# Four buffers instead of two for the stored expert activations that a transformer block reads back

## The chip, the cores and the metric

The kernel runs on one core of one Trainium2 chip. The metric is the device time of one execution in microseconds (us), as a median over runs; the span of a profile is the time from the first to the last instruction on the core. The core has five engines that run at the same time and meet only through semaphores: TensorE (PE: matmuls, with its weight loads shown as PEld), VectorE (DVE), ScalarE (ACT), GpSimd (POOL) and SyncE (SP, which here only issues transfers). Each engine, and each queue on which an engine issues transfers (SPq, POOLq), works strictly in its own order: an instruction that waits holds up everything behind it.

## The reference, cut to what matters

One layer of a hybrid encoder on 512 tokens of width 1024: two kinds of attention, then a feed-forward part made of 16384 single-neuron experts of which each token picks 8 x 16, then a gated embedding. The change touches the expert part alone:

```python
def peer_ffn(h, w_query, sub_keys, expert_u, expert_v):   # h: 512 x 1024
    ...                                                   # scores, top 16 per head -> eidx, g
        u = jnp.take(expert_u, eidx, axis=0)
        a = jnp.einsum('thkd,td->thk', u, hc).astype(jnp.float32)
        act = (jax.nn.gelu(a, approximate=False) * g).astype(hc.dtype)
        vv = jnp.take(expert_v, eidx, axis=0)
        return jnp.einsum('thk,thkd->td', act, vv)
```

## The kernel before

The first 128 tokens are done as the reference writes it: GpSimd gathers rows of `peer_expert_u` and `peer_expert_v` (`experts0`, L920 to L951; tile `gath`, three buffers), and VectorE does one fused multiply per gathered tile. This work runs beside everything else.

The other 384 tokens are done densely, over 128 blocks of 128 experts. For one block b:

- *up* (`up`, L1010 to L1021): 24 matmuls give the pre-activations `aT` (128 experts x 384 tokens), from the block of `uT` (512 KB, load L130, split into a rounded high part by ScalarE L141 and a low part `wl` by VectorE L143). ScalarE applies Gelu into a tile `ge`.
- *act* (`act`, L1130 to L1144): VectorE multiplies the activations by the block's gate matrix `G` (L1139), ScalarE rounds the product (`ahi`, L1141), VectorE takes the rest (`alo`, L1143). `ahi` and `alo` have three buffers each. `G` comes from DRAM for four blocks at a time (768 KB, L1133, two buffers).
- *down* (`down`, L1146 to L1154): 18 matmuls (L1153) of `ahi` and `alo` with the block of `peer_expert_v` (512 KB, load L130, split in the same way into `vh` by ScalarE and `vl` by VectorE; two raw and three split buffers), summed up over all 128 blocks in six PSUM banks `out`.

The gate matrices are not ready until late. So the ups of blocks 0 to 75 (`NSP` = 76) are done early, beside the selection work, and their activations are stored to DRAM (`ahead`, L1037; `ge_d`, 192 KB a block). After that a last stage, called the **fused stage** here, goes through all 128 blocks in the order of the list `order` (L1023): groups of four *fresh* blocks (up, act, down) alternate with one or two groups of four *stored* blocks, for which the activation is read back from `ge_d` into a tile `gr` (L1136, L1137) and only act and down remain. There are 52 fresh and 76 stored blocks. The act of a block is written one block ahead of its down (list `pend`, L1162).

A tile's tag with `bufs=2` has two places. A load into a place may go out only when the last reader of what lay there is done: for `gr` that is the subtraction L1143 two stored blocks earlier. The program text is not the final order. A planner simulates the kernel, gives each engine and queue a fixed order from its own costs, and sets the semaphores; a load gets its place on SP's queue about where the simulation sees its buffer come free. The loads of the last stage (`gple`, `x3` from `x2_d`, `pl` from `ple_d`; L1184 to L1214) are tied behind the load of `G` that is current twelve blocks before the end (`late`, L1170), so that they come onto SP's queue while the last stored blocks still run.

Of the kernel before, what the change touches and what calls it, by code (L numbers as in the profile page):

```python
# [10 lines left out]
F32 = mybir.dt.float32  # L11
# [53 lines left out]
def block_kernel(ctx: ExitStack, tc: tile.TileContext, a: dict):  # L65
# [26 lines left out]
    def mark(i):  # L92
        latest[:] = [i.ins]
        return i
# [1029 lines left out]
    dn = dns.enter_context(tc.tile_pool(name="dn", bufs=1))  # L1124
# [5 lines left out]
    def act(b, ge):  # L1130
        if b % GB == 0:
            Gs[:] = [dn.tile([128, 384 // TH, GB, TH], F32, tag="G", name="G", bufs=2)]
            loads[:] = [nc.sync.dma_start(Gs[0], g_d[:, :, b:b + GB].rearrange("s p b t -> p s b t")).ins]  # L1133
        G = Gs[0][:, :, b % GB]
        if ge is None:
            ge = dn.tile([128, 384], F32, tag="gr", name="gr", bufs=2)  # L1136
            nc.sync.dma_start(ge, ge_d[b])  # L1137
        gv = ge.rearrange("p (s t) -> p s t", t=TH)
        mark(nc.vector.tensor_mul(gv, gv, G))  # L1139
        ahi = dn.tile([128, 384], F32R, tag="ahi", name="ahi", bufs=3)  # L1140
        nc.scalar.copy(ahi, ge)  # L1141
        alo = dn.tile([128, 384], F32R, tag="alo", name="alo", bufs=3)
        nc.vector.tensor_sub(alo, ge, ahi.bitcast(F32))  # L1143
        return ahi, alo  # L1144
# [11 lines left out]
    def whole(b):  # L1156
        for v in up(b):
            if isinstance(v, float):
                tick(v)
        return v  # L1160

    pend = []  # L1162
    for i, (b, fresh) in enumerate(order):
        if i == GB * HEAD:

            exp_side.rate = left[0] / (sum(3.88 * f + 3.84 for _, f in order[i:]) - EARLY)
        ge = whole(b) if fresh else None
        pend.append(act(b, ge))
        if i == NB - 12:
            late = loads[0]  # L1170
        if len(pend) > 1 and i <= NB - 3:
            run(down(*pend.pop(0), i - 1, V.take(1)))
            V.free()
# [115 lines left out]
```

## Time and profile before

| what | value |
|---|---|
| median of three runs | 1824.28 us (1823.26 to 1829.8) |
| the profiled execution's own time | 1824.99 us |
| span in its profile | 1823.2 us |
| TensorE busy over the span | 1781.7 us (98%) |
| VectorE, ScalarE, GpSimd busy | 1311.8 us (72%), 727.6 us (40%), 537.1 us (29%) |
| fused stage | about 1012 to 1756 us of the span, then the last projection to the end |

Busy time is the time in which an engine executes something. Idle time is listed in front of the instruction that follows it, with what ended it. Matmuls overlap in TensorE's pipeline, so that the duration of one (0.39 us in the fused stage) is longer than the distance between two.

### The profile page before, as it was taken

To read this page: it belongs to the slowest core of one execution; us is meant where nothing else is said; L and a number is where in the kernel's file an instruction comes from. 1 tells how busy PE (TensorE), PEld (TensorE's weight loads), DVE (VectorE), ACT (ScalarE), POOL (GpSimd) and SP (SyncE) were. 2 spreads that over 40 slices of the span, in tenths; PEclk is the share of its full clock that TensorE was granted. 3 is DMA by queue.
4 is the path that set the end of the run, shared out by engine and by line. 5 is a ranking of instruction groups with operands and counts; after the bars stand their busy time and mean duration, and the time that the engine had idled before them with its cause. 6 is when DMAs were issued, how large, how long until landed. Compare 5 with 4: busy or idle time off the path is not lost.

```text
span 1823.2 us, 26237 instructions
## 1 busy us (share of the span) xinstructions
PE 1781.7 (98%) x9613; PEld 1562.5 (86%) x9613; DVE 1311.8 (72%) x2638; ACT 727.6 (40%) x1202; POOL 537.1 (29%) x428
## 2 busy tenths in 40 slices
PE   8999999999899899999999999999999999999998
PEld 6997777788788799999999988888787888888787
DVE  6634644436568899998998678777786887778664
ACT  4434553443333545444444433333333333333342
POOL 4201111112434121132452134333343433344200
PEclk9999999999899999999999999999999999999999
DMA  5231124334312576788888989898898999899922
GB/s 183 81 92 35 47 54 127 93 108 135 127 47 93 187 265 196 258 276 324 307 323 329 363 317 342 320 334 325 299 338 309 329 349 331 318 329 327 354 98 81
DMA packets 159537, 417.12 MB, mean 229 GB/s; under 512 B 14128, under 2 KB 61488, under 8 KB 156336
## 3 DMA queue, kind: packets, MB, share of 16 engines
q1 hardware_dynamic: 122112, 279.64, 44.3%
q0 software_dynamic: 36864, 134.23, 20.3%
q8 instruction: 75, 1.23, 0.3%
q10 hardware_dynamic: 432, 1.57, 0.2%
q14 instruction: 54, 0.44, 0.1%
HBM read 368.73 MB, written 45.88 MB: 227 GB/s over the span
## 4 chain that ended last, share of the span: by engine, by line
PE 75%; DMA 11%; issue 6%; DVE 4%; POOL 2%; ACT 1%; SPq 0%; POOLq 0%; DVEq 0%; ACTq 0%
PE out L1153 14%; PE aT L171 8%; PE aT L172 8%; PE aT L173 8%; DMA gath<-peer_expert_v,eidx 4%; PE gp L1103 4%; PE proj L171 3%; DMA gr<-ge_d 3%; PE proj L172 3%; PE proj L173 3%; POOL gath L932 2%; PE gt L173 2%; PE gt L171 2%; PE gt L172 2%; PE qp L171 2%
## 5 line engine op out<-in xcount | busy, mean ns | idle before, releaser
L171 PE MATMUL aT<-hhi,wh 128*128 128x384 f32 x1024 | 345.7, 338 | 4.8 <-ACT ge L1020 4.8
L173 PE MATMUL aT<-hhi,wl 128*128 128x384 f32 x1024 | 345.0, 337 | 0.0
L172 PE MATMUL aT<-hlo,wh 128*128 128x384 f32 x1024 | 344.7, 337 | 0.0
L141 ACT CAST wh<-wr 128x1024 fp32r<-128x1024 f32 x216 | 226.8, 1052 | 238.2 <-PE aT L172 160.8
L932 POOL DMA_INDIRECT gath<-peer_expert_u,eidx x128 | 185.9, 1453 | 434.0 <-DVE gath L943 292.5
L143 DVE TENSOR_TENSOR wl<-wr,wh 128x1024 fp32r<-128x1024 f32 x184 | 228.2, 1241 | 107.0 <-ACT wh L141 104.5
L932 POOL DMA_INDIRECT gath<-peer_expert_v,eidx x128 | 197.2, 1541 | 306.8 <-DVE acc L951 224.3
L1153 PE MATMUL out<-vh,ahi 128*128 128x512 f32 x768 | 233.1, 392 | 9.2 <-ACT ahi L1141 9.2
L1153 PE MATMUL out<-vl,ahi 128*128 128x512 f32 x768 | 238.4, 392 | 3.4 <-DVE vl L143 3.3
L1153 PE MATMUL out<-vh,alo 128*128 128x512 f32 x768 | 233.4, 391 | 2.1 <-DVE alo L1143 2.1
L141 ACT CAST vh<-vr 128x1024 fp32r<-128x1024 f32 x128 | 134.4, 1051 | 224.6 <-DMA vr<-peer_expert_v 174.3
L171 PEld LDWEIGHTS aT<-hhi,wh 128*128 128x128 f32 x1024 | 193.0, 189 | 8.1 <-ACT ge L1020 5.2
L951 DVE SCALAR_TENSOR_TENSOR acc<-gath,act,acc 128x1024 f32<-128x1024 f32 x128 | 163.9, 1280 | 44.1 <-DMA gath<-peer_expert_v,eidx 43.8
L172 PEld LDWEIGHTS aT<-hlo,wh 128*128 128x128 f32 x1024 | 192.9, 188 | 3.0
L173 PEld LDWEIGHTS aT<-hhi,wl 128*128 128x128 f32 x1024 | 192.9, 188 | 1.6
L943 DVE SCALAR_TENSOR_TENSOR gath<-gath,h2n 128x1024 f32<-128x1024 f32 x128 | 155.1, 1219 | 32.0 <-DMA gath<-peer_expert_u,eidx 31.7
L1153 PEld LDWEIGHTS out<-vh,ahi 128*128 128x128 f32 x768 | 143.1, 188 | 37.5 <-ACT ahi L1141 11.3
L1153 PEld LDWEIGHTS out<-vl,ahi 128*128 128x128 f32 x768 | 143.8, 188 | 35.8 <-DVE vl L143 6.0
L149 POOL TENSOR_TENSOR wl<-wr,wh 128x256 fp32r<-128x256 f32 x128 | 99.6, 815 | 250.6 <-ACT wh L141 220.8
L1153 PEld LDWEIGHTS out<-vh,alo 128*128 128x128 f32 x768 | 143.6, 188 | 34.7 <-DVE alo L1143 4.6
L143 DVE TENSOR_TENSOR vl<-vr,vh 128x1024 fp32r<-128x1024 f32 x128 | 156.1, 1220 | 11.8 <-ACT vh L141 11.7
L171 PE MATMUL proj<-wh,hhi 128*128 128x512 f32 (+1 forms) x256 | 108.6, 427 | 6.8 <-ACT wh L141 6.8
(259 smaller groups left out, 2847.0 us busy)
## 6 DMA issues: line engine op xcount, KB each, us to landing
vr<-peer_expert_v SPq DMA_DIRECT2D x128, 512.0 KB
wr<-uT SPq DMA_DIRECT2D x128, 512.0 KB
g_d<-stage SPq DMA_DIRECT2D x24, 1024.0 KB
G<-g_d SPq DMA_DIRECT2D x32, 768.0 KB
wr<-w_in SPq DMA_DIRECT2D x46, 512.0 KB
ge_d<-ge SPq DMA_DIRECT2D x76, 192.0 KB
gr<-ge_d SPq DMA_DIRECT2D x76, 192.0 KB
wr<-peer_w_query SPq DMA_DIRECT2D x16, 512.0 KB
```

What stands on the lines that cost most here:

```text
L141: nc.scalar.copy(hi, self.raw[i])
L143: nc.vector.tensor_sub(lo, self.raw[i], hi.bitcast(F32))
L149: nc.gpsimd.tensor_sub(l[:, cs], r[:, cs], h[:, cs].bitcast(F32))
L171: nc.tensor.matmul(ps, st[0], mv[0], start=start, stop=False)
L172: nc.tensor.matmul(ps, st[0], mv[1], start=False, stop=False)
L173: nc.tensor.matmul(ps, st[1], mv[0], start=False, stop=stop)
L932: nc.gpsimd.indirect_dma_start(out=t, out_offset=None, in_=a["peer_expert_" + kind], in_offset=bass.IndirectOffsetOnAxis(ap=eidx[:, c:c + ...
L943: nc.vector.scalar_tensor_tensor(t, t, 1.0, h2n, op0=ALU.mult, op1=ALU.mult, accum_out=a0[:, c:c + 1])
L951: nc.vector.scalar_tensor_tensor(acc0, t, act0[:, c:c + 1], acc0, op0=ALU.mult, op1=ALU.add)
L1103: nc.tensor.matmul(gpb[:, 128 * x:128 * x + 128], o[:, 1, cs], m[:, s, cs], start=(s == 0), stop=(s == 2))
L1153: nc.tensor.matmul(outs[t][h], w[:, cs], x[:, h], start=first and p == 0, stop=last and p == 2)
```

## The change

The tag of the tile `gr` gets four places instead of two. Nothing else in the program text differs; the planner runs again over the whole kernel. A place takes 1.5 KB of each partition, so the pool `dn` grows by 3 KB a partition.

```diff
         if ge is None:
-            ge = dn.tile([128, 384], F32, tag="gr", name="gr", bufs=2)
+            ge = dn.tile([128, 384], F32, tag="gr", name="gr", bufs=4)
             nc.sync.dma_start(ge, ge_d[b])
```

## Rows read from the trace of the kernel before

**Rows 1.** Windows: busy us (x instructions) per engine, granted clock, DMA share, GB/s
```profile
core 0: us, PE busy (x) PEld busy (x) DVE busy (x) ACT busy (x) POOL busy (x), PEclk, DMA share, GB/s
1012.00:1756.00 744.00, 729.33 (x3453) 631.41 (x3452) 571.76 (x737) 265.72 (x367) 271.02 (x199) 1.00 0.91 325
```
**Rows 2.** Waits of TensorE, fused stage: waiter <- releaser, total us, times, longest
```profile
PE out L1153 <- ACT ahi L1141: 9.2, 6, 3.1
PE out L1153 <- DVE vl L143: 3.3, 4, 1.5
PE out L1153 <- DVE alo L1143: 2.1, 2, 1.6
```
**Rows 3.** Waits of VectorE in the fused stage
```profile
DVE gr L1139 <- DMA gr<-ge_d: 63.8, 29, 9.8
DVE acc L951 <- DMA gath<-peer_expert_v,eidx: 39.8, 24, 3.9
DVE gath L943 <- DMA gath<-peer_expert_u,eidx: 25.6, 17, 3.2
```
**Rows 4.** Timeline of VectorE, 1278 to 1285 us: start, us, what [idle before]
```profile
1277.56 0.55 DVE L1143 TENSOR_TENSOR alo<-gr,ahi 128x384 fp32r<-128x384 f32 x1
...
1284.57 0.56 DVE L1139 TENSOR_TENSOR gr<-gr,G 128x384 f32<-128x384 f32 x1 [4.77 <-DMA gr<-ge_d]
```
**Rows 5.** Timeline of SP's queue, same stretch
```profile
1278.14 0.33 SPq L1137 DMA_DIRECT2D gr<-ge_d  x1
```
**Rows 6.** Waits of SP's queue in the fused stage
```profile
SPq L130 <- DVE vl L143: 296.0, 118, 7.4
...
SPq L1137 <- DVE alo L1143: 68.7, 37, 7.8
```
**Rows 7.** Chain that ended last: start, us, what
```profile
1045.46 4.12 PE out L1153 x18
```
**Rows 8.** Timeline of TensorE: three of its twelve waits in the stage
```profile
1229.10 0.73 PE L1153 MATMUL out<-vh,alo 128*128 128x512 f32 x2 [0.50 <-DVE alo L1143]
...
1465.19 0.73 PE L1153 MATMUL out<-vh,ahi 128*128 128x512 f32 x2 [0.97 <-ACT ahi L1141]
...
1697.35 0.75 PE L1153 MATMUL out<-vh,ahi 128*128 128x512 f32 x2 [3.06 <-ACT ahi L1141]
```
**Rows 9.** Timeline of VectorE: multiplies that waited ahead of those three
```profile
1223.66 1.03 DVE L1139 TENSOR_TENSOR gr<-gr,G 128x384 f32<-128x384 f32 x2 [2.01 <-DMA gr<-ge_d]
...
1464.03 0.56 DVE L1139 TENSOR_TENSOR gr<-gr,G 128x384 f32<-128x384 f32 x1 [3.87 <-issue]
...
1696.14 0.56 DVE L1139 TENSOR_TENSOR gr<-gr,G 128x384 f32<-128x384 f32 x1 [9.77 <-DMA gr<-ge_d]
```
**Rows 10.** Timeline of SP's queue near the end of the stage
```profile
1643.15 1.99 SPq L1137 DMA_DIRECT2D gr<-ge_d  x2
...
1678.41 1.69 SPq L1191 DMA_DIRECT2D x<-x_d  x3
1680.20 1.01 SPq L1137 DMA_DIRECT2D gr<-ge_d  x1
```
**Rows 11.** Timeline of TensorE after the longest wait
```profile
1697.91 1.04 PE L1153 MATMUL out<-vl,ahi 128*128 128x512 f32 x2
...
1701.31 0.63 PE L1153 MATMUL out<-vh,alo 128*128 128x512 f32 x2
```
**Rows 12.** Windows of short stretches, columns as in the first group
```profile
1698.00:1700.00 2.00, 2.00 (x6) 1.55 (x5) 1.29 (x3) 1.00 (x2) 1.01 (x1) 0.50 0.48 150
...
1509.00:1524.00 15.00, 15.00 (x70) 12.74 (x69) 9.75 (x12) 3.44 (x5) 3.42 (x5) 1.00 0.94 335
...
1250.00:1292.00 42.00, 41.29 (x192) 34.81 (x191) 29.55 (x44) 13.55 (x20) 12.53 (x10) 1.00 0.83 296
1479.00:1509.00 30.00, 30.00 (x150) 26.88 (x149) 27.54 (x41) 13.06 (x19) 13.14 (x10) 1.00 1.00 372
```
**Rows 13.** Waits of ScalarE in the fused stage
```profile
ACT vh L141 <- DMA vr<-peer_expert_v: 174.3, 63, 8.8
```

## The prediction

> **What bounds the kernel now.** I read the page first (TensorE busy 98% of the span), then the windows of the fused stage, the only place where a tile `gr` exists. Of its 744 us TensorE is idle for 744 - 729.33 = 14.67 us [rows 1]. The waits say what that idle time is: matmuls of the down projection that wait for `ahi`, `vl` or `alo`, 9.2 + 3.3 + 2.1 = 14.6 us in 6 + 4 + 2 = 12 places [rows 2]. So the stage is bound by TensorE, and what better buffering can give is bounded: 14.67 us, 0.8% of the kernel, plus what a wait costs after it has ended (below). The reader should set against it the third view, VectorE's waits: 63.8 us in 29 places for a load of `gr`, its largest wait, ahead of the gathers' 39.8 and 25.6 us [rows 3]. Most of these 63.8 us cost nothing now, since act runs a block ahead of down; the whole question is which of the twelve places stand behind them.
>
> The fourth view shows why VectorE waits. A subtraction of an older stored block ends at 1277.56 + 0.55 = 1278.11 us [rows 4]; the load goes out at 1278.14 [rows 5]; the multiply that needs it stands ready from 1279.80 and starts at 1284.57, after 4.77 us idle [rows 4]. The load takes about 6.4 us from issue to use and could not go out sooner, because its place was full. It is the rule: SP's queue stood 37 times, 68.7 us in all, at a load of `gr` until a subtraction had freed the place [rows 6]; 76 such loads, taken in pairs, have 38 occasions.
>
> **The change, part by part.**
>
> *Lead of the load.* A down is 18 matmuls in 4.12 us [rows 7]. With two places a load leads its use by two stored blocks, 2 x 4.12 = 8.2 us, less what passes between a block's multiply and the end of its subtraction (0.56 and 0.55 us [rows 4], and ScalarE's cast and other work between them; I estimate 2 us in all): some 6 us, against a load that takes 6.4 us and more. With four places the lead is 4 x 4.12 = 16.5 us, some 14 after the same deduction. In a group of four stored blocks all four loads can go out during the fresh blocks before it; in a pair of groups the first four can. The 29 waits should nearly all go.
>
> *What of that is on TensorE's path.* I followed each of the twelve waits back through VectorE and ScalarE. Behind six of them stands a late `gr`: the multiply came after a wait of its own, and `ahi`, `alo` or `vl` queued behind it came late for TensorE. The six are 0.50, 0.71, 0.97, 0.57, 0.44 and 3.06 us, in order of time (the first, third and sixth are shown [rows 8]), sum **6.25 us**; the waits of 2.01, 3.87 and 9.77 us on VectorE belong to the three shown [rows 9]. The one of 3.87 us is labelled as issue time; I count it, as it stands at a multiply of a `gr` whose load had just been freed. The other six, 14.6 - 6.25 = 8.35 us, stand behind late loads of `vr`, late gathers or late `G`; I count nothing for them and keep 8.35 us as the bound.
>
> *The longest one.* The load that went out at 1680.20 us was queued on SP behind three loads of `x3` [rows 10] and was used only at 1696.14, 15.9 us later [rows 9]. With four places it is freed where the pair at 1643.15 us was [rows 10], well before `x3` is issued. What is late next? The load two blocks on takes its place behind `x3` and lands around 1696 us; TensorE wanted the first at 1697.35 - 3.06 = 1694.29 [rows 8] and will want that one 2 x 4.12 = 8.2 us later, at 1702.5. Its act needs an estimated 2 us, so about 4 us are left over. I take the whole 3.06.
>
> *The clock after it.* The granted clock was 0.50, the 1.2 GHz level, from 1698 to 1700 us [rows 12], right after TensorE had stood for 3.06 us. Eight matmuls took 1701.31 - 1697.91 = 3.40 us [rows 11]; at 4.12 / 18 each they take 1.83. So that wait cost **1.57 us** more. The five other waits of the six are under 1 us; I charge them nothing.
>
> *Sum.* 6.25 + 1.57 = 7.8 us. The profiled execution took 1824.99 us, 1.79 above its span and 0.71 above the median of the runs; a difference carries over, so 1824.28 - 7.8 = **1816.5 us**. At the most 14.67 + 1.57 = 16.2 us, 1808.0; from below nothing, or a loss (rivals).
>
> *What it adds.* No instruction and no byte. At the stage's start four loads go out at once instead of two, 2 x 192 KB = 0.39 MB more ahead of the others, at 325 GB/s [rows 1] 1.2 us. I take nothing, since the same bytes leave the stretches in which stored blocks run; bound 1.2 us if that cover is gone. The pool's 3 KB shift later tiles; their loads would have to move by far more than these 15 us to matter at the end of the stage. Nothing.
>
> *A rule against my bound.* In a stretch without any wait, 1509 to 1524 us, weight loads are busy for 12.74 of 15 us, 85% [rows 12], and in the whole stage for 631.41 of 744, again 85% [rows 1]. The Trainium skill (Perfetto Trace Analysis, Identifying the Most-Contended Engine) says that busy matmul time is a poor measure of the room left, and that the busy share of weight loads is a good one. By that the room would be 744 - 631.41 = 112.6 us, and the time could fall to 1711.7. The trace does not bear that out: 85% is what it shows where TensorE waits for nothing.
>
> **The rivals.**
>
> *More goes than the six.* VectorE, freed of up to 63.8 us, does its part of the gathers and the splits sooner, `vr` is loaded sooner, and the other waits shrink too. For it: SP's loads wait 296 us for VectorE's `vl` [rows 6]. Against: those waits come from transfers in part, and an earlier VectorE then waits for them. With half of the 8.35 us more: 1816.5 - 4.2 = 1812.3; with all of it 1808.
>
> *No change.* The transfers are the limit: the loads of `gr` come earlier, those of `vr`, `G` and the gathers correspondingly later, and TensorE waits as before; or the planner leaves the loads where they are. 1824, give or take 3. For it: the 16 engines are 0.91 busy over the stage [rows 1], 1.00 at 372 GB/s in one stretch [rows 12], and ScalarE already waits 174.3 us for `vr` [rows 13]. Against: from 1250 to 1292 us, where VectorE stood still for 4.77 us at one `gr` alone [rows 4], the engines were only 0.83 busy [rows 12]: there a place was lacking and not bandwidth. The Trainium skill (HBM Reference, Specifications (TRN2)) gives about 358 GB/s as a core's share when both of a pair stream, and 425 alone. By the first the stage would be 91% full, which is the rival; the 372 GB/s of the trace are above it.
>
> *Slower.* The planner puts the loads of `gr` further ahead on SP's queue than VectorE frees their places on the chip, and `vr` and `wr` wait behind them. The price is the time in which SP stands at such a load, now 37 times for 68.7 us [rows 6], of which TensorE's waits for `vl`, 3.3 us [rows 2], are all that can be seen. If the gain stays, the kernel gets slower by over 0.5% once 9.1 + 7.8 = 16.9 us of it reach TensorE, a quarter. With a third, 22.9 us, it takes 1816.5 + 22.9 = 1839. Against: a place four blocks old is freed earlier than one two blocks old, and the five buffers of `v` cover short stops.
>
> **How the numbers follow.** A measurement of this kernel tells about 0.5%, 9.1 us, from no change, so faster is below 1815.2 and slower above 1833.4. The forecast (a gain of 3 to 9.1 us, 1815.2 to 1821) 0.45; more than the six, past 9.1 us, 0.28; no change 0.15; slower 0.10; the 112.6 us 0.02. Faster 0.28 + 0.02 = 0.30, same 0.45 + 0.15 = 0.60, slower 0.10. The range goes from 1808, the bound of the gain, to 1829, the no-change case with its runs' spread; it leaves out the slower case and the 112.6 us, 0.12.
>
> **What the profile after would show.** VectorE's wait for loads of `gr` falls from 63.8 us to under 15. Waits on SP's queue at L1137 remain, but at places four blocks old. TensorE's idle time in the fused stage falls from 14.67 to about 8 us, the wait of 3.06 near 1697 us and the stretch at half clock behind it are gone, and the six others remain. I am wrong if the waits for `gr` go and TensorE's idle time stays (no change), if new waits for `vl` or `wl` appear behind loads that SP held up (slower), or if the order of other instructions comes out so differently that the twelve places cannot be found again.

## The result, and the profile after

The kernel with four places takes **1807.12 us** (median of 4 runs, 1804.0 to 1809.38) against 1826.38 us (4 runs, 1823.26 to 1829.8) for the kernel before on the same chip: ratio **0.988**, 95% interval 0.9858 to 0.9903, a gain of about 19 us. That is below the forecast of 1816.5 us and just below the range (1808 to 1829). The profiled execution took 1807.68 us with a span of 1805.7; the one of before took 1824.99.

The windows of the fused stage, columns as in [rows 1]. The window is 18 us shorter and holds the same 3453 matmuls as the 744 us of before:

```profile
1012.00:1738.00 726.00, 723.57 (x3453) 631.50 (x3452) 573.52 (x737) 265.85 (x366) 254.85 (x199) 1.00 0.93 333
1690.00:1700.00 10.00, 10.00 (x46) 8.34 (x45) 7.69 (x9) 2.84 (x5) 3.24 (x4) 1.00 1.00 375
```

TensorE's idle time in it is 726.00 - 723.57 = 2.43 us, against 14.67. The second line covers the time at which before had its longest wait and the clock of 0.50 [rows 12]. The same work comes up to 18 us earlier now, but neither is found anywhere in the stage: its longest wait is 1.1 us, and the trace has no stretch at 0.50 in it. The first down starts at 1025.1 us (1024.7 in before), and from the last one to the end it is 55 us in both, so that the whole gain lies in this stage. Waits of TensorE, VectorE, SP's queue and ScalarE (waiter <- releaser: total us, times, longest), for [rows 2, 3, 6, 13]:

```profile
PE out L1153 <- ACT ahi L1141: 2.4, 3, 1.1
```
```profile
DVE vl L143 <- ACT vh L141: 35.1, 27, 7.4
DVE wl L143 <- ACT wh L141: 30.4, 24, 2.9
DVE acc L951 <- DMA gath<-peer_expert_v,eidx: 30.2, 22, 4.9
...
DVE gath L943 <- DMA gath<-peer_expert_u,eidx: 15.0, 16, 2.3
...
DVE gr L1139 <- DMA gr<-ge_d: 7.4, 8, 2.0
```
```profile
SPq L130 <- DVE vl L143: 257.1, 120, 7.2
SPq L1137 <- DVE alo L1143: 127.2, 53, 7.8
```
```profile
ACT vh L141 <- DMA vr<-peer_expert_v: 156.3, 58, 7.6
```

VectorE's waits for `gr` went from 63.8 to 7.4 us, those for gathers from 65.4 to 45.2. VectorE now waits for ScalarE's high parts instead. TensorE waits in 3 places instead of 12, each time for ScalarE's `ahi`, and no longer for VectorE's `vl` or `alo`. SP's queue stands *longer* at loads of `gr` than before (127.2 against 68.7 us), and the stage is shorter all the same.

But two things changed at once: the tile has four places, and the planner wrote a new order for TensorE, VectorE, ScalarE and SP's queue. SP's queue after, in the first stored blocks of a pair of groups (start, us, what), has three loads of `gr` out within 7.5 us, and they stand *ahead* of loads of `vr`:

```profile
1246.80 0.38 SPq L1133 DMA_DIRECT2D G<-g_d  x1
1248.88 3.44 SPq L1137 DMA_DIRECT2D gr<-ge_d  x2
1253.13 0.33 SPq L130 DMA_DIRECT2D vr<-peer_expert_v  x1
1255.89 0.32 SPq L1137 DMA_DIRECT2D gr<-ge_d  x1
1257.55 0.33 SPq L130 DMA_DIRECT2D vr<-peer_expert_v  x1
```

### The profile page after: what moved, and what is told of

Its sections match the earlier page's. It is cut to its first block, busy times and chain, and to the rows that moved or that the text cites. A ratio compares the mean times of both kernels' runs of the same rounds, so it can differ in the third digit from the quotient of the medians.

```text
span 1805.7 us, 26185 instructions
## 1 busy us (share of the span) xinstructions
PE 1774.1 (98%) x9613; PEld 1561.1 (86%) x9613; DVE 1314.0 (73%) x2638; ACT 727.4 (40%) x1202; POOL 525.8 (29%) x428
## 3 DMA queue, kind: packets, MB, share of 16 engines
q10 hardware_dynamic: 432, 1.57, 0.2%
## 4 chain that ended last, share of the span: by engine, by line
PE 91%; DMA 4%; DVE 2%; ACT 1%; issue 1%; SPq 0%; POOL 0%; ACTq 0%; DVEq 0%; POOLq 0%
PE out L1153 27%; PE aT L171 9%; PE aT L173 9%; PE aT L172 9%; PE proj L171 3%; PE proj L172 3%; PE proj L173 3%; PE gp L1103 3%; DMA g_d<-stage 2%; PE gt L173 2%; PE gt L171 2%; PE gt L172 2%; DMA vr<-peer_expert_v 2%; PE qp L171 2%; PE qp L172 2%; PE qp L173 2%
## 5 line engine op out<-in xcount | busy, mean ns | idle before, releaser
L932 POOL DMA_INDIRECT gath<-peer_expert_u,eidx x128 | 181.4, 1417 | 435.9 <-DVE gath L943 296.9
L932 POOL DMA_INDIRECT gath<-peer_expert_v,eidx x128 | 191.4, 1495 | 302.3 <-DVE acc L951 213.5
```

The source lines that it names most:

```text
L932: nc.gpsimd.indirect_dma_start(out=t, out_offset=None, in_=a["peer_expert_" + kind], in_offset=bass.IndirectOffsetOnAxis(ap=eidx[:, c:c + ...
```

## Experiments

Five theories were to be told apart. **Lead**: the loads go out earlier, VectorE no longer waits for them. **Depth**: not the loads, but the products `gr`·`G` can run further ahead. **Traffic**: the bytes of the read-back are what costs. **Order**: the planner's new order would gain by itself. **Supply of `vr`**: its loads limit the stage, and `gr` is only in their way. Ratios are against the kernel before on the same chip, with 95% intervals.

| run | median us (runs) | before | ratio |
|---|---|---|---|
| e1 three load places, own product tile with two | 1813.12 (6) | 1827.28 | 0.9915 (0.9884 to 0.9946) |
| e2 one load place, four products | 1816.31 (7) | 1827.28 | 0.9927 (0.9899 to 0.9955) |
| e3 no read-back, two products | 1823.85 (12) | 1827.28 | 0.9969 (0.9948 to 0.999) |
| e4 three places | 1811.82 (6) | 1827.28 | 0.9895 (0.9863 to 0.9926) |
| e5 four places, old order everywhere | 1831.88 (12) | 1829.78 | 1.0004 (0.998 to 1.0028) |
| e6 four places, old order on VectorE | 1820.37 (10) | 1829.78 | 0.9939 (0.9913 to 0.9966) |
| e7 no read-back, four products | 1841.08 (12) | 1829.78 | 1.0042 (1.0016 to 1.0069) |
| e8 five places | 1806.46 (6) | 1829.78 | 0.9869 (0.9824 to 0.9913) |
| e9 four places, old order on SP's queue | 1826.46 (12) | 1826.66 | 0.9994 (0.9979 to 1.0009) |
| e10 old order, 8 KB loads | 1810.97 (4) | 1826.66 | 0.9899 (0.9876 to 0.9921) |
| e11 `vr` three places, `gr` two | 1841.96 (6) | 1826.66 | 1.007 (1.0049 to 1.0092) |
| e12 `vr` three places, `gr` four | 1829.78 (12) | 1826.66 | 1.0011 (0.9992 to 1.0029) |
| e13 four places, old order but loads two earlier | 1813.71 (6) | 1830.3 | 0.9907 (0.988 to 0.9934) |
| e14 old order, full loads that nobody waits for | 1810.98 (6) | 1830.3 | 0.9899 (0.9871 to 0.9926) |
| e15 the same with 8 KB loads | 1806.51 (6) | 1830.3 | 0.9871 (0.9843 to 0.9899) |

### Splitting the tile, and leaving the load out (e1 to e4, e7, e8)

The load tile `gr` and the product got tiles of their own, with R and P places:

```diff
-            ge = dn.tile([128, 384], F32, tag="gr", name="gr", bufs=2)
+            ge = dn.tile([128, 384], F32, tag="gr", name="gr", bufs=R)
             nc.sync.dma_start(ge, ge_d[b])
+            gq = dn.tile([128, 384], F32, tag="gq", name="gq", bufs=P)
+        else:
+            gq = ge
...
-        mark(nc.vector.tensor_mul(gv, gv, G))
+        ge = gq
+        mark(nc.vector.tensor_mul(ge.rearrange("p (s t) -> p s t", t=TH), gv, G))
```

*e1: R = 3, P = 2.*

> Loads of the stored activations go into three places, the product with G goes into a tile of its own with two places, so a load's place is free as soon as the multiply is done, but only two products can lie ready. Lead theory (the gain came from loads that go out earlier, so that VectorE no longer waits for them): 1806 to 1812 us, VectorE's wait for these loads under 15 us. Depth theory (the gain came from products that lie ready in four places, some 22 us ahead of their matmuls instead of 9, so that any wait of VectorE or ScalarE is absorbed): two products as before, 1818 to 1825 us, whatever the wait for loads. Order theory (the planner's new order of instructions happened to be a good one): anywhere between 1800 and 1830 us, with no relation to either.

Measured 0.9915 (1813.12 us, just above the 1806 to 1812 that I had given to lead; VectorE's waits for `gr` are 7.7 us): a faster kernel with only two products. Depth is not needed.

*e2: R = 1, P = 4.*

> The opposite: one place for the load, four for the product. Each load goes out only when the multiply before it is done. Lead theory: VectorE waits 6 us or so at many of the 76 loads, 1826 to 1850 us. Depth theory: the products are made far ahead wherever the transfers allow it, 1807 to 1815 us in spite of long waits of VectorE. Order theory: anywhere between 1800 and 1830 us.

Measured 0.9927, where lead expected no gain. VectorE's waits for `gr` were 36.5 us in 18 places, against 63.8 in 29: with a product tile of its own the one load place is freed by the multiply and no longer by the subtraction behind it, so that the load did come earlier than I had reckoned. By itself e2 doesn't decide between lead and depth.

*e3: no load, P = 2; e7: no load, P = 4.* The multiply reads a tile that is there anyway:

```diff
-            ge = dn.tile([128, 384], F32, tag="gr", name="gr", bufs=2)
-            nc.sync.dma_start(ge, ge_d[b])
+            gq = dn.tile([128, 384], F32, tag="gq", name="gq", bufs=P)
+            gv = h2n[:, 0:384].rearrange("p (s t) -> p s t", t=TH)
+            ge = gq
...
-        mark(nc.vector.tensor_mul(gv, gv, G))
+        mark(nc.vector.tensor_mul(ge.rearrange("p (s t) -> p s t", t=TH), gv, G))
```

> The stored activations are not read back at all: the 76 stored blocks multiply G with a tile that lies ready (other data, so this part of the computation is changed), into two places for the product. 14.6 MB of loads and every wait for them are gone. Lead theory: at or below the changed kernel, 1800 to 1808 us. Depth theory: the six waits of TensorE that stood behind late vr, G and gathers remain, 8.35 us, so 1813 to 1820 us. Order theory: between 1800 and 1830 us.

> As the run without any read-back (other data in the stored blocks' multiplies), but with four places for the product instead of two. Depth theory: products far ahead absorb VectorE's waits for gathers and G, 1803 to 1810 us, against 1824 with two. Lead theory has no reason for a change against the run with two places: 1818 to 1828 us.

Both missed: 0.9969 and 1.0042. Without a load of `gr` nothing can wait for one, and yet e7 is *slower* than before. TensorE's waits in e7, of which `vl` has most:

```profile
PE out L1155 <- DVE vl L143: 11.3, 13, 2.6
PE out L1155 <- ACT ahi L1143: 6.3, 4, 3.2
```

What follows is a warning: each of these kernels got an order of its own. e15 below has two product places like e3, takes the same waits and nearly all of the same bytes out of the *old* order, and gains 1.3%, where e3 gained 0.3%. So the order is likely to be worth nearly as much as the effect I was after. This is not shown: the orders are the main difference between e3 and e15, but no run changed the order alone, and which instruction of e7's order does the harm was not traced.

*e4: three places; e8: five.* The change's own line with `bufs=3` and `bufs=5`.

> Three places, all else as before. Lead theory and depth theory: between the two kernels, 1812 to 1820 us, VectorE's wait for the loads some 20 to 40 us. Order theory: no order by the number of places, so it may lie outside the two, under 1804 or over 1830 us.

> Five places. With four, TensorE is idle for 2.4 us of the fused stage, so nothing much is left: 1804 to 1809 us by lead and depth theory alike. If the result depends on the accident of one planned order rather than on the number of places, it may as well come out at 1815 us or more.

0.9895 and 0.9869: with four at 0.988 the three cannot be told apart. One more place already does it, though VectorE's waits for `gr` fell only to 26.5 us there, and there is no version that clearly beats the change.

### Holding the order (e5, e6, e9, e13)

Now the instructions get order-only edges that put them into the order of the kernel before (`ORDER`, a list of instruction names for each engine and queue that is held); data and buffers are as in the change. In the traces of e5 and e13 every instruction stands where it stood in before in its engine's order, but for the transfers that e13 moves on SP's queue.

```diff
+    known = {i.name: i for i in nc.cur_bb.bb.instructions}
+    for names in json.loads(zlib.decompress(base64.b85decode(ORDER))).values():
+        names = [n for n in (f"I-{x}" for x in names) if n in known]
+        for before, after in zip(names, names[1:]):
+            tc.add_manual_dep(known[after], before, mybir.DependencyInfo(mybir.DependencyClass.NoSync,
+                                                                         mybir.DependencyReason.DATA), reason="order")
```

*e5: all engines and queues.*

> Four places, but on every engine and queue the instructions stand in exactly the order of the kernel before, so only the waits for places are gone. Lead theory, and the working of the prediction: a load goes out earlier by what SP's order leaves it, the six waits of TensorE behind late loads go, 1816 to 1820 us. Order theory, in its new form (most of the gain comes from the order that the planner can make once there are four places, not from loads that wait less): little is left, 1821 to 1828 us, and VectorE's wait for the loads stays above 30 us. If it comes out at 1810 or less, the new order is not needed at all.

1.0004: **four places without a new order do nothing.** The waits of VectorE and of TensorE, and the windows:

```profile
DVE gr L1139 <- DMA gr<-ge_d: 63.4, 30, 11.0
```
```profile
PE out L1153 <- ACT ahi L1141: 11.2, 8, 4.9
PE out L1153 <- DVE vl L143: 6.4, 6, 1.9
PE out L1153 <- DVE alo L1143: 2.1, 4, 0.9
```
```profile
1012.00:1756.00 744.00, 724.06 (x3409) 624.26 (x3408) 564.94 (x728) 261.43 (x360) 273.29 (x199) 0.99 0.90 322
```

The reason stands in SP's queue and on VectorE:

```profile
1281.04 0.33 SPq L130 DMA_DIRECT2D vr<-peer_expert_v  x1
1281.42 0.43 SPq L1137 DMA_DIRECT2D gr<-ge_d  x1
1283.79 0.33 SPq L130 DMA_DIRECT2D vr<-peer_expert_v  x1
1284.17 1.30 SPq L1137 DMA_DIRECT2D gr<-ge_d  x1
```
```profile
1283.68 0.55 DVE L1143 TENSOR_TENSOR alo<-gr,ahi 128x384 fp32r<-128x384 f32 x1
1284.15 0.17 DVE L949 TENSOR_TENSOR act<-ge,gate 128x16 f32<-128x16 f32 x1
1289.00 0.56 DVE L1139 TENSOR_TENSOR gr<-gr,G 128x384 f32<-128x384 f32 x1 [4.68 <-DMA gr<-ge_d]
```

It is the scene of [rows 4, 5] again, though the place had long been free: over the stage the median load went out 12.7 us after its place was (0.03 us in before). It stands in the queue behind a load of `vr`, and that one waits until VectorE's `vl` has freed its own place.

*e9: SP's queue alone; e6: VectorE alone; all else planned anew.*

> Four places, SP's queue alone held to the order of the kernel before, so that each load of a stored activation stays behind the same load of vr; VectorE, ScalarE and TensorE are planned afresh around it. If the gain needs the loads to go out earlier: ratio to the kernel before 0.996 to 1.004. If VectorE's and TensorE's new order is worth something by itself: 0.987 to 0.994.

> Four places, VectorE alone held to the order of the kernel before, all other engines and queues planned afresh around it. If the gain comes from what VectorE does earlier (multiplies of stored blocks far ahead of their matmuls): little gain, 1818 to 1828 us. If it comes from SP's earlier loads or from TensorE's order: 1806 to 1814 us.

With the old order on SP's queue the gain is gone (0.9994, VectorE waits 69.2 us for `gr`). With the old order on VectorE, and SP free, it stays in part (0.9939, and no wait for `gr`). In us e6 lies in the range that I had given to VectorE's part, but before ran at 1829.78 us on that chip. So SP's order is needed for the gain; how much VectorE's new order adds, e6 leaves open, and e13 answers it.

*e13: the old order everywhere, but in SP's list each load of `gr` stands where the load two earlier stood.*

> Four places and the order of the kernel before on every engine and queue, with one thing moved: on SP's queue each load of a stored activation stands where the load two blocks earlier stood (the first three go out together). Every other instruction keeps its place. If earlier loads are the whole gain: VectorE's wait for them under 15 us, ratio to the kernel before 0.986 to 0.992, as with the plain change. If the planner's new order of VectorE, ScalarE and TensorE is half of it: 0.992 to 0.996. If the waits were only worth what the prediction counted, 7.8 us: 0.995 to 0.997.

0.9907: in the order in which four places alone did nothing (e5), moving the 76 loads up by two positions, and nothing else, brings 1830.3 - 1813.71 = 16.6 us. The loads' earlier issue is nearly all of the gain, with VectorE's order kept. The median load now leads the moment at which its multiply is ready by 19.2 us (7.0 in before), the shortest by 11.9 (1.7). No wait of VectorE for `gr` is left. TensorE's waits and the window:

```profile
PE out L1153 <- DVE vl L143: 3.0, 2, 2.3
PE out L1153 <- ACT ahi L1141: 2.5, 4, 0.9
PE out L1153 <- ACT vh L141: 1.9, 1, 1.9
PE out L1153 <- DVE alo L1143: 0.2, 1, 0.2
```
```profile
1012.00:1756.00 744.00, 736.35 (x3495) 639.99 (x3494) 573.07 (x739) 266.96 (x368) 270.26 (x199) 1.00 0.92 326
```

### Waits against bytes, in the old order (e10, e14, e15)

e10 cuts the load to 16 of 384 columns and, against what I expected of it, keeps the waits; e14 keeps the load whole, but the product is made from other data, so that nobody waits for it; e15 does both:

```diff
-            nc.sync.dma_start(ge, ge_d[b])
+            gr = dn.tile([128, 384], F32, tag="gr", name="gr", bufs=2)
+            nc.sync.dma_start(gr[:, 0:W], ge_d[b, :, 0:W])
+            ge = dn.tile([128, 384], F32, tag="gq", name="gq", bufs=2)
+            gs = h2n[:, 0:384]
+        else:
+            gs = ge
...
-        mark(nc.vector.tensor_mul(gv, gv, G))
+        mark(nc.vector.tensor_mul(gv, gs, G))
```

(W = 384 in e14, 16 in e15; e10 has `gr` as the product tile, too, and W = 16, so that its multiply, which overwrites the tile, still waits for the load.)

> Two places and exactly the order of the kernel before, but each of the 76 loads brings 16 of its 384 columns, and the multiply takes other data in place of the stored activation (so this part of the computation is changed). This takes VectorE's wait for these loads away and leaves everything else where it was: the term of the prediction measured by itself. By the prediction's working 7.8 us less than before, ratio 0.994 to 0.998. If the waits for these loads cost nothing, because VectorE then waits for gathers instead: 0.998 to 1.002. If they held up more than the six places: under 0.992.

> Two places and exactly the order of the kernel before; all 76 loads with all their bytes go out where they stood, but nothing reads them: the multiply takes other data (so this part of the computation is changed) and writes to a tile of its own with two places. This takes away VectorE's waits for the loads and no byte. If the waits are the cost: ratio 0.984 to 0.992. If the 14.3 MB on the transfer engines were what the run with 16 columns gained by: 0.997 to 1.003.

> The same with 16 of 384 columns in each load that nothing reads: neither wait nor bytes, in exactly the order of the kernel before (this part of the computation is changed again). If the planner's own order was what made the two runs without any read-back no faster, this one is fast: ratio 0.982 to 0.990. If it is 0.996 or more, something else in the old order holds the fused stage at its length.

e14: 0.9899. **Taking the waits away, with every byte kept, gives 1%**, as much as e13. Two waits went with one edit, VectorE's for the load and SP's for a subtraction that frees the place (68.7 us in before, none in e14); e13 has the same gain with 64.8 us of SP's left. TensorE's waits in e14, and the window:

```profile
PE out L1157 <- ACT vh L141: 3.5, 1, 3.5
PE out L1157 <- DVE vl L143: 2.3, 2, 1.4
PE out L1157 <- DVE alo L1147: 2.2, 3, 0.9
PE out L1157 <- ACT ahi L1145: 2.0, 3, 0.9
```
```profile
1012.00:1756.00 744.00, 733.76 (x3477) 636.57 (x3477) 572.77 (x739) 266.12 (x368) 272.71 (x199) 1.00 0.91 325
```

(This profiled execution took 1819.08 us, 8.1 above the run's median.) e15 gives 0.9871; that the bytes add something is likely from the medians, but the intervals overlap. e10 gave 0.9899 in a way that I had not expected: the waits were supposed to vanish with the bytes, and they did not.

```profile
DVE gr L1142 <- DMA gr<-ge_d: 49.1, 24, 7.0
```

So 49.1 of 63.8 us of waits were left, and TensorE was idle for 4.9 us only:

```profile
1012.00:1756.00 744.00, 739.10 (x3516) 642.87 (x3515) 576.38 (x750) 269.26 (x372) 269.31 (x200) 1.00 0.87 306
```

Fewer bytes thus bring a gain of the same size with most of the waits left. Traffic can't be what the change saves, since it moves the same bytes, but it is a second way to the same 1%; the two together give 1.3% (e15). With 306 GB/s over the stage, against 325, `vr` landed 6.0 us after its issue and `G` 7.7, against 6.7 and 9.2 in e14. My reading, which no run tests by itself: when the other transfers are less late, a VectorE that waits for `gr` reaches TensorE less often.

### More raw places for `vr` (e11, e12)

```diff
-    V = Stream(None, "v", 2, 3, gel)
+    V = Stream(None, "v", 3, 3, gel)
...
-        T = big.tile([128, NG, 5, OG, 2], BF16, tag="iT", name="iT", bufs=2)
+        T = big.tile([128, NG, 5, OG, 2], BF16, tag="iT", name="iT", bufs=1)
```

e12 has `gr` with four places in addition (and one place for `hn`, to make room).

> Two places for the stored activations as before, but three raw places instead of two for the blocks of peer_expert_v (one tile of the stage before, iT, gets one place instead of two to make room). If what TensorE waits for in the end is the supply of vr, with the stored activations only in its way: 1803 to 1812 us. If the stored activations' two places are the limit: 1818 to 1828 us.

> Four places for the stored activations and three raw places for peer_expert_v (iT and, in the last stage, hn get one place instead of two to make room). With TensorE idle for only 2.4 us of the fused stage in the changed kernel, at most 3 us are left, and the last stage may lose 1 to 3 us with one hn: 1804 to 1811 us by every theory; over 1815 would mean that the planner's order is the larger term.

Both totals (1.007 and 1.0011) are spoilt by the room I took: with one place for `iT` the stage *before* grew, and the first down starts at 1040.8 and 1038.0 us instead of 1024.7. Within the fused stage the reading is plain. In e11 ScalarE's waits for `vr` fell from 174.3 to 42 us, and the stage took as long as before (743.0 us from the first down to the last, 743.5 in before). The medians agree: e11 is 15.3 us above before, and its first down comes 16.1 us later. With four places for `gr` in the same build (e12) the stage takes 730.8 us, and the median is 12.2 us below e11's. With two places for `gr` the supply of `vr` is not the limit.

## Why the prediction was wrong

**What held.** The stage is bound by TensorE, late loads of `gr` hold up VectorE, and the gain is in their lead (e13, e14). The waits for `gr` fell below 15 us (7.4), those on SP's queue at L1137 stayed (127.2 us), the wait of 3.06 us and the half clock behind it are gone. The no-change rival through transfers fell: the same bytes pass in 18 us less, at 333 GB/s instead of 325. The slower rival fell: SP stands 58.5 us longer at loads of `gr`, and TensorE's waits for `vl` are gone. The rule on weight loads (the Trainium skill, Perfetto Trace Analysis, Identifying the Most-Contended Engine) would have allowed 112.6 us. The trace does not bear it out: their share went to 631.50 of 726.00, 87%, with TensorE all but never idle, and no run here took more than about 24 us off its kernel before.

**The step that failed is the term put at nothing: the other six waits of TensorE, 8.35 us, for which I counted nothing because their last cause was not a load of `gr`.** With it failed the sum, 7.8 us, and the bound of 16.2: the earlier loads alone are worth 16.6 us (e13) and the change 19.3. In the profile after, TensorE's idle time fell by 12.24 us, not by 6.25. Points 1 and 3 below and unlisted idle time made the sum too small; point 2 works the other way.

*1. The split into six and six.* I followed each wait back to one last cause and counted those at a late `gr`. In e5 and in e13 to e15 TensorE has before's order, so the matmuls can be matched by number. In e13 all six that I counted are gone. But the other six, which were to stay at 8.35 us, fell too: of 0.70, 1.49, 1.52, 1.56, 1.47 and 1.59 us there remain 0, 0, 0.88, 0.82, 2.26 and 0.24, sum 4.20. In e14, where only the waits at `gr` went, 0.65 and 1.37 remain (seven new ones came up there, 7.9 us in all, the longest 3.51), and in e15 1.12. Chance has a part in this: in e5, where nothing got faster, the same six have 6.10 us in place of 8.33. The six that I had counted have 7.39 us there in place of 6.25, and none in e13 to e15. So at least a part of the other six, and by e14 and e15 most, stood behind `gr`, too. The way there, a VectorE that had lost time earlier and was late for gathers, splits and `G`, is argued and was not followed wait by wait. That is my rival "more goes than the six", which I had given 0.28; its top, 1808, is nearly the result.

*2. What comes in their place.* e13 has four places that before did not have: 0.60, 0.79, 0.20, and 1.86 us at the down just after the one that had waited for 3.06. These make a gain smaller and not larger; the sum had nothing for them. I had taken the whole 3.06 us, with "about 4 us left over", and looked only at the next load of `gr`. ScalarE's cast there waits for `vr` (idle in brackets):

```profile
1696.02 1.04 ACT L141 CAST vh<-vr 128x1024 fp32r<-128x1024 f32 x1 [5.86 <-DMA vr<-peer_expert_v]
```

Together 4.20 + 3.45 = 7.65 us: nearly the 8 us forecast for the profile after, by two errors of opposite sign, which is luck. In after itself 2.43 are left.

*3. One execution of before, taken as the kernel.* With idle time at 7.65 us, e13's profile is where the prediction put it, and its execution (1817.36 us) is 7.6 us below before's (1824.99). The medians say 16.6. The rest is where each profiled execution lies among the runs: before's was 5.31 us under the median of before's runs on e13's chip (1830.3, eleven other runs), e13's was 3.65 over its own (1813.71), and 7.63 + 5.31 + 3.65 = 16.59. For the change itself this is a small part: from profile to profile it gains 17.3 of the 19.3 us. e5 is as good as a second execution of before, in the same order and at the same speed: it shows 18 waits and 19.94 us idle where [rows 1] show 14.67, only nine of the twelve places in common, and 4.89 us where [rows 8] show 3.06. A bound read from 14.67 us was no bound of the median.

*And idle time is not the price of a wait.* A matmul's modelled end lies later than the next one could have started. Ahead of the wait of 3.06 us stands

```profile
1693.95 0.34 PE L171 MATMUL aT<-hhi,wh 128*128 128x384 f32 x1
```

and the next starts at 1697.35 [rows 8], 3.40 us later, where 0.17 is usual between starts: the wait cost 3.23 us and not 3.06. Measured from start to start, the twelve waits cost 16.56 us instead of 14.58, the three of after 2.93 instead of 2.43. Short delays of 60 to 150 ns, which the waits do not list at all, come on top (22 in before, 2.36 us; 7 in after, 0.74), as does the half clock, 1.59 us, close to the 1.57 reckoned. 13.6 + 1.6 + 1.6 = 16.8 of the 18 us that separate the two profiles; the rest I can't assign.

**What else was off.** The lead: 6 us with two places and 14 with four was the estimate. The medians are 7.0 us in before and 9.1 in after, where the planner also moved the multiplies; only e13, with VectorE's order kept, shows what four places allow, 19.2. In before 37 of 76 loads led by under 7 us, in after 14, in e13 none. But the lead is not all: e5 has a median of 9.1, too, and 24 loads under 7, and VectorE waits as long as in before. Where it waited there, the load was used 8.7 us after its issue (median), against 6.9 in before; why it took longer was not traced. The 38 pairs of loads don't fit the trace of before, where only 23 loads follow another directly, but the reading does: 71 of the 74 loads that had to wait for a place go out within 0.1 us after it is free. And "the planner leaves the loads where they are" was put under no change as a side remark; e5 and e9 show that the change hangs on exactly this.

**What stays open.** Whether after's new order adds anything to the moved loads: its profile has 2.43 us idle against e13's 7.65, but the ratios 0.988 and 0.9907 have overlapping intervals. An order may well matter by this much (e3 against e15). And how the gain of e10 divides into shorter waits and lighter traffic.

## What to carry to other kernels

A further buffer only frees a place; it gains when the queue that issues the load also issues it earlier, so look at what stands ahead of it in that queue, and hold the order fixed when the two are to be told apart. When an engine in the middle waits often, don't count only the stalls that lead straight back to that wait: it makes the engine late for what comes after, and stalls with other labels can go with it. And take the size from several executions, by distances between starts: here the listed idle time fell by 12.2 us where the medians fell by 19.3.

## What was unexpected of the hardware

- A small load behind large ones is hardly faster. In e10 the issues of SP's queue (KB each, median us from issue to landing) are these:

```profile
vr<-peer_expert_v SPq DMA_DIRECT2D x126, 512.0 KB, 6.0
...
gr<-ge_d SPq DMA_DIRECT2D x76, 8.0 KB, 6.0
```

  8 KB take as long as the 512 KB they follow. Of the two runs that differ in nothing else, e14 has 8.6 us for 192 KB and e15 7.5 for 8 KB. Whether the transfers ahead hold the small load up, or that it goes as 128 packets of 64 bytes, was not told apart.
- Executions of one program spread a good deal: before took 1820.49 to 1840.9 us in 27 runs on one chip. In the fused stage the profile of before has one stretch at a granted clock of 0.50, e5, in the same order, two.
